# One plain group of heads instead of two, a second norm that ends later, and a rotation on folded rows, in a four-stage decoder step

## The chip, the core and the metric

The kernel runs on one core of a Trainium2 chip. The metric is device time of one execution, in microseconds: the median of repeated runs, with the lowest and highest. One further execution was taken with the hardware profiler, and all rows quoted come from it. PE is the matrix engine (TensorE), PEld its weight loads, DVE the vector engine, ACT the scalar engine, POOL GpSimd, SP the queue that issues most DMAs.

## The reference

One inference step of a two-layer decoder with a shared key/value projection between the layers: 1024 prompt positions and 8 single-position samples, model width 2048, all in float32.

```
# layer 0 (mixer A), for prompt and samples
z = x @ w_in_a;  u, gate = split(z)
d = multiscale_pool(u)                      # trailing means over 2, 4, 8, 16 positions, minus u
d = einsum('btgc,gce->btge', d, w_grp_a) * scale
h = layer_norm(ALPHA * x + (d * silu(gate)) @ w_out_a)
# shared keys and values, once
k, v = split(h @ w_kv);  k = rope_partial(k)        # first 16 of 64 dims of each head
# layer 1 (mixer B)
z = h @ w_in_b;  q = rope_partial(z[..., :2048]);  gate = z[..., 2048:]
s = q k^T / 8, masked to a sliding window of 128;  softmax with one learned sink per head
y = layer_norm(ALPHA * h + (softmax(s) v * silu(gate)) @ w_out_b)

rope_partial: out = [x1*cos - x2*sin, x2*cos + x1*sin, rest]      # x1, x2: 8 dims each
```

It returns y for prompt and samples, the pooling states, and the last 128 keys and values.

## The kernel before

**Layout.** Activations lie with channels on the 128 partitions and positions along the free axis. The positions are cut into two chunks: chunk 0 has 512, chunk 1 has 520 (512 and the 8 samples). Every stage is run for chunk 0 and then for chunk 1, in the order of the table `PHASES`: `ai` (projection, pooling, gate), `ao` (output projection and norm), `bi` (keys, values, queries, gates, attention), `bo` (output projection and norm).

**Products.** A float32 product is made of three reduced-precision ones: each weight block and each activation tile is split into a high half (a cast on ACT, L505 for weights) and a low half (a subtraction on DVE, L520), and PE adds high x high, high x low, low x high (L684, L685, L686). A stage multiplies in one of two ways. *Plain* (`unit`, L712 to L714): 48 matmuls of 512 columns for 128 output channels. *By seven* (`pair` and `seven`): two tiles of output channels at a time, by the Strassen-Winograd scheme, in seven products of 24 matmuls with half the columns (256 or 260). These seven need sums of weight blocks (a block of a pair of input tiles is 128 x 1024) and of activations. Weight sums are formed on DVE (L349) by `first_pair`, which in chunk 0 also stores them to DRAM (`swib`, by POOL, L351) for chunk 1, where `next_pair` loads them. The sums of activations are four DVE operations, `t_ops` (L895 to L898), stored by POOL (L899) as `th` for the norm's output and `to` for the attention's.

**The stage that changes.** `bi` for chunk 0, from 1077.1 to 1508.0 us. It first makes keys and values and the first two groups of heads plain (a group is two tiles of query channels and two of gate channels: four plain units or two pairs by seven), then six groups by seven. While it runs plain, the norm of `ao` for chunk 1 (`ln_gen`, c = 1) is done as side work: mean, then subtraction (L1031), squares (L1034) and their sums (L1037) for each of eight tiles of 2 x 520 columns, then a second pass that multiplies (L1071), applies gain and offset on ACT (L1060), stores `h`, and forms and stores the activations' sums `th`. The eight tiles stay in SBUF between the two passes. In chunk 1 the pairs in `FORM` (groups 0 and 1, whose sums chunk 0 never needed) form their sums themselves and do not store them.

**Rotation.** `w_kv` and `w_in_b` are permuted so that the two rotated halves of a head lie 32 partitions apart. `partner` copies a tile (or pair of tiles) into another with the 32-row blocks exchanged (four SP DMAs), and `rope` multiplies both by tables (L1740), and the sum is formed at L1848, all on the full 128 partitions and all columns.

**Attention** (`attend`) of one query tile is a chain of small steps hung on products that come later: scores (L1879), select (L1896), mask and maximum (L1900, L1904), exponentials (L1915), normalisation (L1928), transposes (L1932), copies (L1941, L1942), values (L1957), gate (L1966) and its store `o` (L1969), and for every second tile the `t_ops` and their store.

**What sets the order.** Every engine runs its instructions in the order in which the source records them (`in_order`). Time in the source is counted in products: `begin` opens one and `end` closes it, `self.at(n, go)` and `self.product(n, rank, go)` record `go` at the end of the n-th product from now, and one step of side work is taken there if enough memory is free (`every`, `room`). `begin` also keeps the weights ahead: it loads seven entries ahead, casts four and forms low halves for three, counted with the one that is opened, so that low halves lie two products ahead of PE:

```
a, b, d = self.ahead if self.strassen else (5, 4, 3)      # ahead = 7, 4, 3
self.load_to(self.e + a);  self.prep_to(self.e + d);  self.cast_to(self.e + b)
```

**Memory.** SBUF beyond the constants is one pool of 54 slots (`Mem`) of a block or a pair of tiles each. `full` and `half` take the whole slot that was released longest ago; a slot whose content was stored counts as ten releases younger. A writer of a slot waits until its last reader is done, a store by DMA too.

## Time and profile before

| | |
|---|---|
| median of 3 runs | 2302.97 us (2302.83 to 2305.52) |
| the profiled execution, its span | 2307.35 us, 2305.6 us |
| PE, DVE, ACT, POOL busy | 2281.9, 1942.7, 1388.5, 192.3 us |
| TensorE clock granted | 0.999 |
| `bi` chunk 0, plain part | 1077.1 to 1221.5 us: 144.4 us, PE 144.40, DVE 120.39 |
| `bi` chunk 0, by seven | 1221.5 to 1508.0 us: 286.5 us, PE 286.04, DVE 257.76 |
| `bi` chunk 1 begins | 1508.0 us |

A row of a group reads: line, engine, operation, output tile <- input tiles with their shapes, count, then busy us and mean ns of one, then the engine's idle time just before it and what ended it. A row of the waits reads: who waited, for whom, us in total, how many times, the longest. A tile named `m` is a slot of the pool, `pD`, `pS`, `pO` are PSUM banks.

### The profile page before, as it was taken

How to read it: one execution, taken by the hardware profiler on the slowest of the kernel's cores; microseconds unless marked ns; L12 is line 12 of the kernel's file. 1: busy time of each engine (PE TensorE's matmuls, PEld its weight loads, DVE VectorE, ACT ScalarE, POOL GpSimd, SP SyncE). 2: the span in 40 equal slices, each digit the busy share in tenths (PEclk: the TensorE clock that was granted, in tenths of full speed). 3: DMA queues.
4: the chain of work that ended last, by engine and by line, in shares of the span. 5: the costliest groups of instructions: out<-in, count | busy, mean ns of one | idle time of the engine just before them, and what ended most of it. 6: DMA issues, size and time to landing. Idle time of an engine off the chain costs nothing.

```text
span 2305.6 us, 50389 instructions
## 1 busy us (share of the span) xinstructions
PE 2281.9 (99%) x20353; PEld 2211.4 (96%) x20353; DVE 1942.7 (84%) x2415; ACT 1388.5 (60%) x2547; POOL 192.3 (8%) x359
## 2 busy tenths in 40 slices
PE   9999999999999999999999999999999999999998
PEld 8999999999999999999889999999999999999998
DVE  8888889877878878988878989899877777889997
ACT  5544446544546546555466776785766778656665
POOL 0111110011010000000001111100000000010001
PEclk9999999999999999999999999999999999999999
DMA  7779679988889989999667767787787778799894
GB/s 257 264 267 309 233 255 325 318 303 295 298 308 320 345 294 317 321 352 383 214 255 252 241 226 239 264 285 231 230 264 234 252 239 293 244 364 379 289 339 151
DMA packets 246394, 648.31 MB, mean 281 GB/s; under 512 B 25200, under 2 KB 106000, under 8 KB 246160
## 3 DMA queue, kind: packets, MB, share of 16 engines
q1 hardware_dynamic: 204288, 493.13, 64.1%
q0 software_dynamic: 41872, 151.96, 17.0%
q8 instruction: 159, 2.61, 0.5%
q14 instruction: 75, 0.61, 0.1%
HBM read 463.00 MB, written 172.47 MB: 276 GB/s over the span
## 4 chain that ended last, share of the span: by engine, by line
PE 54%; DVE 2%; DMA 2%; ACT 1%; issue 1%; SPq 0%; POOL 0%; DVEq 0%; POOLq 0%; ACTq 0%
PE pD L684 14%; PE pD L686 13%; PE pD L685 13%; PE pD L712 2%; PE pO L1957 2%; PE pD L714 2%; PE pD L713 2%; PE pS L1879 2%; PE pS L1932 1%; DMA m<-in_woa 1%; DVE m L520 1%; DMA h<-m 0%; DMA m<-swob 0%; PE pS L1957 0%; PE pO L684 0%
## 5 line engine op out<-in xcount | busy, mean ns | idle before, releaser
L684 PE MATMUL pD<-m,m 128*128 128x260 f32 (+1 forms) x5088 | 1440.6, 283 | 5.8 <-ACT pD L644 2.3
L686 PE MATMUL pD<-m,m 128*128 128x260 f32 (+1 forms) x5088 | 1433.4, 282 | 5.3 <-DVE m L520 5.2
L685 PE MATMUL pD<-m,m 128*128 128x260 f32 (+1 forms) x5088 | 1433.6, 282 | 0.0
L684 PEld LDWEIGHTS pD<-m,m 128*128 128x128 f32 x5088 | 958.3, 188 | 15.3 <-issue 6.2
L686 PEld LDWEIGHTS pD<-m,m 128*128 128x128 f32 x5088 | 958.8, 188 | 7.4 <-DVE m L520 7.4
L685 PEld LDWEIGHTS pD<-m,m 128*128 128x128 f32 x5088 | 958.0, 188 | 0.5
L520 DVE TENSOR_TENSOR m<-m,m 128x1024 fp32r<-128x1024 f32 x690 | 833.4, 1218 | 93.4 <-ACT m L505 37.9
L505 ACT CAST m<-m 128x1024 fp32r<-128x1024 f32 x690 | 720.8, 1049 | 264.2 <-DVE m L349 127.5
L349 DVE TENSOR_TENSOR m<-m,m 128x1024 f32<-128x1024 f32 x136 | 166.1, 1221 | 13.1 <-DMA m<-in_wia 10.7
L847 DVE TENSOR_TENSOR m<-m,m 128x1024 fp32r<-128x1024 f32 (+1 forms) x118 | 143.8, 1224 | 7.3 <-ACT m L838 5.7
L838 ACT CAST m<-m 128x1024 fp32r<-128x1024 f32 (+1 forms) x118 | 123.3, 1052 | 9.7 <-DVE m L520 3.9
L657 ACT COPY m<-pD 128x260 f32<-128x260 f32 (+1 forms) x88 | 32.9, 374 | 118.2 <-PE pD L686 117.9
L1915 ACT ACTIVATE m<-m,sm 128x128 f32<-128x128 f32 x256 | 99.3, 391 | 0.0
L645 DVE TENSOR_TENSOR m<-pD,m 128x260 f32<-128x260 f32 (+1 forms) x92 | 38.3, 416 | 69.9 <-ACT pD L644 63.8
L1181 PE MATMUL pD<-m,m 128*128 128x260 f32 (+1 forms) x528 | 91.5, 323 | 0.0
L623 ACT ACTIVATE pD<-pD 128x260 f32<-128x260 f32 (+1 forms) x90 | 33.3, 370 | 93.6 <-PE pD L686 93.3
L712 PE MATMUL pD<-m,m 128*128 128x512 f32 x224 | 89.1, 398 | 0.0
L714 PE MATMUL pD<-m,m 128*128 128x512 f32 x224 | 88.2, 394 | 0.0
L713 PE MATMUL pD<-m,m 128*128 128x512 f32 x224 | 88.1, 393 | 0.0
L1181 PEld LDWEIGHTS pD<-m,m 128*128 128x128 f32 x528 | 79.4, 188 | 8.2
L1928 ACT ACTIVATE m<-m,sm 128x128 f32<-128x128 f32 x256 | 81.9, 392 | 7.0 <-DVE sm L1923 6.3
L632 ACT COPY m<-pD 128x260 f32<-128x260 f32 (+1 forms) x92 | 34.3, 373 | 77.4 <-PE pD L686 77.2
(257 smaller groups left out, 2096.3 us busy)
## 6 DMA issues: line engine op xcount, KB each, us to landing
m<-in_wib SPq DMA_DIRECT2D x132, 512.0 KB
m<-in_wia SPq DMA_DIRECT2D x128, 512.0 KB
m<-swoa SPq DMA_DIRECT2D x64, 512.0 KB
swia<-m POOLq DMA_DIRECT2D x56, 512.0 KB, 4.7
m<-swia SPq DMA_DIRECT2D x56, 512.0 KB
m<-swob SPq DMA_DIRECT2D x56, 512.0 KB
m<-in_wob SPq DMA_DIRECT2D x52, 512.0 KB
m<-in_woa SPq DMA_DIRECT2D x48, 512.0 KB
```

The lines of the kernel that those rows point to most:

```text
L349: self.nc.vector.tensor_add(s[out].a[:, :1024], s[x].a[:, :1024], s[y].a[:, :1024])
L505: self.nc.scalar.copy(hi.r[:, :1024], self.stream[self.cast].src().a[:, :1024])
L520: self.nc.vector.tensor_sub(lo.r[:, :1024], s.src().a[:, :1024], hi.a[:, :1024])
L684: nc.tensor.matmul(ps[:, :TH], wh[:, s], h, start=new and k == 0, stop=False, skip_group_check=on)
L685: nc.tensor.matmul(ps[:, :TH], wh[:, s], l, start=False, stop=False, skip_group_check=on)
L686: nc.tensor.matmul(ps[:, :TH], wl[:, s], h, start=False, stop=k == 7, skip_group_check=on)
L712: nc.tensor.matmul(ps[:], wh[:, s], h, start=par == 0 and k == 0, stop=False)
L713: nc.tensor.matmul(ps[:], wh[:, s], l, start=False, stop=False)
L714: nc.tensor.matmul(ps[:], wl[:, s], h, start=False, stop=par == 1 and k == 7)
L838: self.nc.scalar.copy(h.r[:, :n], s.a[:, :n])
L847: self.nc.vector.tensor_sub(l.r[:, :n], s.a[:, :n], h.a[:, :n])
L1181: nc.tensor.matmul(ps[:, : cs.stop - cs.start], ws[:, s], d[:, cs], start=f0 and k == 0, stop=l0 and k == 3,)
```

## The change

It does the following.

- `PHASES`: plain in `bi` of chunk 0 are now only keys, values and group 0; seven groups go by seven. Group 1 there forms its weight sums and stores them, and in chunk 1 it loads them (`FORM` holds group 0 alone).
- `ln_gen` for chunk 1: after a tile has been centred and squared, it is stored (`p`) and its slot released; the second pass loads it again, and waits until the stage runs by seven. There it takes a step at every second product at most, if four slots are free.
- Rotation: the 16 rotated rows of each of the two heads in a tile are written to DRAM (SP), read back folded, so that eight pieces of the columns and eight rows lie on 64 partitions (SP), turned by three DVE operations on 128 x 256 elements, written back to DRAM (POOL), and read back into the tile (SP), at products 0, 1, 3 and 5 after the tile is done (0, 1, 2, 4 for the last). The permutation within a head is dropped, the tables are folded too. Keys are then copied by ACT.
- Scores, and all that hangs on them, come two products later; two decode steps three later, and decode scores lie elsewhere in the bank.
- `begin` keeps fewer entries ahead when fewer than three slots are free (in `bi`; fewer than five in `bo` of chunk 0).
- `acc` of `phase_out` is taken when it is first needed; the next stage's activations are begun in the last unit of values.

```diff
-    ("ai", 0, (0, 1)), ("ai", 0, (1, 8)), ("ai", 1, (0, 8)), ("ao", 0, None), ("ao", 1, None), ("bi", 0, (0, 2)),
-    ("bi", 0, (2, 8)), ("bi", 1, (0, 8)), ("bo", 0, None), ("bo", 1, None),
+    ("ai", 0, (0, 1)), ("ai", 0, (1, 8)), ("ai", 1, (0, 8)), ("ao", 0, None), ("ao", 1, None), ("bi", 0, (0, 1)),
+    ("bi", 0, (1, 8)), ("bi", 1, (0, 8)), ("bo", 0, None), ("bo", 1, None),
...
-FORM = (0, 1)
+FORM = (0,)
...
-DEC_AT = (0, 1, 6, 6, 7, 8, 9, 10, 13, 13), (11, 11, 12, 12, 13, 14, 15, 16, 17, 17)
+ROPE_AT = (0, 1, 3, 5), (0, 1, 2, 4)
+DEC_AT = (3, 4, 6, 6, 7, 8, 9, 10, 13, 13), (11, 11, 12, 12, 13, 14, 15, 16, 17, 17)
...
-        if getattr(self, "ph", "") == "bi1" and len(self.mem.whole()) < 3:
-            a, b, d = min(a, 6), min(b, 3), min(d, 2)
+        if getattr(self, "ph", "") in ("bi0", "bi1", "bo0") and len(self.mem.whole()) < (5 if self.ph == "bo0" else 3):
+            a, b, d = min(a, 5 if self.ph == "bo0" else 6), min(b, 3), min(d, 2)
...
                 if 1 <= p <= 8:
                     sqs[p - 1] = sq if p == 1 else self.mem.full(2 * T)
                     nc.scalar.activation(flat(sqs[p - 1]), flat(pre[p - 1]), AF.Square)
+                    nc.gpsimd.dma_start(away(p - 1), self.pair_view(pre[p - 1], T))
+                    pre.pop(p - 1).free(True)
...
+        while c == 1 and not self.strassen:
+            yield
...
+        if c == 1:
+            load(0)
+            yield
+            for p in range(8):
+                t = self.pair_view(pre[p], T)
+                nc.vector.tensor_mul(t, t, b2(rr))
+                affine(p)
+                load(p + 1)
+                yield
+                self.t_ops(t[:, 0], t[:, 1], td, p, T // 2)
+                pre[p].free(True)
+                yield
+            L.free()
+            return
...
+    def rope(self, s, n, T, last=False):
...
+        def out():
+            for j in range(2):
+                nc.sync.dma_start(rows[j], s.a[64 * j : 64 * j + 16, :N])
+
+        def take():
+            w = box["w"] = self.mem.half(4 * C)
+            for j in range(2):
+                nc.sync.dma_start(w.v(2, C)[64 * j : 64 * j + 64], packed[j])
+
+        def turn():
...
+            nc.vector.tensor_mul(y, x, tab[:, None, :C].to_broadcast([P, 2, C]))
+            nc.vector.tensor_mul(x, x, tab[:, C : 3 * C].rearrange("p (h c) -> p h c", h=2))
+            nc.vector.tensor_add(y, y, x[:, ::-1, :])
+            for j in range(2):
+                nc.gpsimd.dma_start(packed[j], y[64 * j : 64 * j + 64])
+
+        def back():
+            box.pop("w").free(True)
+            for j in range(2):
+                nc.sync.dma_start(s.a[64 * j : 64 * j + 16, :N], rows[j])
+
+        for k, go in zip(ROPE_AT[last], (out, take, turn, back)):
+            self.at(k, go)
...
-                at, s1, ticks = (12 + 7 * n, {12: 11, 13: 9}.get(t, 12), SPREAD) if t < 14 else (
-                    11 + 7 * n, {14: 10, 15: 8}[t], CLOSE
+                at, s1, ticks = (14 + 7 * n, {12: 11, 13: 9}.get(t, 12), SPREAD) if t < 14 else (
+                    13 + 7 * n, {14: 10, 15: 8}[t], CLOSE
...
+            elif (kind, c) == ("bi", 0):
+                self.every, self.room = 2, 4
```

In the rows that follow a slot of the pool is `m`, its number, then how many slots had been handed out and a running number: two names with the same first number are the same memory. First DVE in `bi` of chunk 0, by seven, where the attention's sums `to` of a pair of tiles (L895 to L898, now L898 to L901) are written into a slot that POOL then stores. Before, from the last of the four:

```order
L898 TENSOR_TENSOR m31_1870_16612<-m12_1845_16289,m31_1870_16612 128x256
L520 TENSOR_TENSOR m41_1873_16628<-m29_1851_16343,m17_1869_16584 128x1024
L1900 COPY_PREDICATED m47_1871_16622<-cst_76,pS_215_13088 128x1024
L1904 TENSOR_REDUCE sm_298_16658<-m47_1871_16622 128x8
L1907 SCALAR_TENSOR_TENSOR sm_299_16659<-sm_298_16658,prm_75 128x8
L1908 TENSOR_TENSOR sm_300_16660<-sm_299_16659,prm_75 128x8
L520 TENSOR_TENSOR m0_1877_16674<-m23_1861_16458,m19_1874_16630 128x1024
L349 TENSOR_TENSOR m23_1861_16458<-m23_1861_16458,m29_1851_16343 128x1024
L520 TENSOR_TENSOR m31_1882_16716<-m5_1854_16383,m43_1878_16676 128x1024
```

and now, from the norm's sums `th` (the last two of whose four operations are shown) to the rotation:

```order
L900 TENSOR_TENSOR m25_1834_16200<-m36_1750_15047,m25_1834_16200 128x260
L901 TENSOR_TENSOR m25_1834_16200<-m36_1750_15047,m25_1834_16200 128x260
L523 TENSOR_TENSOR m53_1838_16214<-m23_1811_15883,m19_1831_16089 128x1024
L523 TENSOR_TENSOR m21_1839_16216<-m28_1825_16034,m24_1837_16212 128x1024
L352 TENSOR_TENSOR m28_1825_16034<-m28_1825_16034,m23_1811_15883 128x1024
L2005 SCALAR_TENSOR_TENSOR m32_1816_15920<-pO_283_16147,m30_1746_15009 128x512
L898 TENSOR_TENSOR m0_1841_16249<-m32_1816_15920 128x256
L899 TENSOR_TENSOR m0_1841_16249<-m32_1816_15920 128x256
L900 TENSOR_TENSOR m0_1841_16249<-m32_1816_15920,m0_1841_16249 128x256
L901 TENSOR_TENSOR m0_1841_16249<-m32_1816_15920,m0_1841_16249 128x256
L523 TENSOR_TENSOR m0_1846_16270<-m11_1818_15965,m25_1840_16218 128x1024
L1939 COPY_PREDICATED m41_1842_16259<-cst_76,pS_215_13092 128x1024
```

Before, slot 31 is written again by the third low half after the sums; now slot 0 is written again by the first, and the norm's sums stand just ahead. The order has this first-after form three times, and the second-after form twice before it.

Second, POOL at the same place: before,

```order
L351 DMA swib12_137<-m5_1803_15730 128x1024
L351 DMA swib12_137<-m12_1800_15690 128x1024
L1969 DMA o0_88<-m17_1794_15636 128x512
L899 DMA to0_85<-m9_1819_15959 128x1024
L351 DMA swib12_137<-m34_1810_15805 128x1024
```

and now:

```order
L902 DMA th1_92<-m25_1834_16200 128x1040
L354 DMA swib12_141<-m28_1825_16034 128x1024
L2008 DMA o0_88<-m32_1816_15920 128x512
L902 DMA to0_85<-m0_1841_16249 128x1024
L1933 MEMSET m41_1842_16259 128x256
L1784 DMA rows3_102<-m30_1843_16262 64x2x128 x2
L354 DMA swib5_134<-m45_1845_16268 128x1024
```

The store of `th` and the rotation's rows have come into the queue around the gate's store `o` and the store of `to`.

Third, ACT at the same place, the casts (L508) of the weights:

```order
L626 ACTIVATE pD_284_16206<-pD_282_16122 128x256
L508 CAST m24_1837_16212<-m28_1825_16034 128x1024
L508 CAST m25_1840_16218<-m11_1818_15965 128x1024
L1967 ACTIVATE m37_1817_15927<-m37_1817_15927,sm_281_15960 128x128 x4
L1935 COPY m41_1842_16259<-pS_215_13092 128x768
L632 COPY m30_1843_16262<-pD_285_16222 128x256
L508 CAST m32_1847_16272<-m28_1825_16034 128x1024
```

The second cast now writes slot 25, from which `th` is being stored, and the third slot 32, from which `o` is; what it casts is the block whose low half DVE writes into slot 0 above.

124 lines of the change are left out of this document (60 added, 64 removed).

## The prediction

> **What bounds the kernel now.** I read the page's head first, then busy time by stage, then the waits of the stage that is changed.
>
> ```profile
> span 2305.6 us, 50389 instructions
> PE 2281.9 (99%) x20353; PEld 2211.4 (96%) x20353; DVE 1942.7 (84%) x2415; ACT 1388.5 (60%) x2547; POOL 192.3 (8%) x359
> ```
>
> TensorE is busy for 2281.9 of 2305.6 us, so only two things can move the time: fewer matmul columns, or PE made to wait. The table by stage shows the first stage's plain units alone, the first output projection (56 products by seven), and then the changed stage's plain part and part by seven, and the first 100 us of its second chunk.
>
> ```profile
> 30.10:52.30 22.20, 22.20 (x97) 1.00 0.50 169
> 750.70:909.90 159.20, 159.20 (x1352) 1.00 0.89 313
> ...
> 1077.10:1221.50 144.40, 144.40 (x834) 116.71 (x833) 120.39 (x152) 81.36 (x155) 12.90 (x25) 1.00 0.74 258
> 1221.50:1508.00 286.50, 286.04 (x3212) 278.68 (x3210) 257.76 (x301) 202.79 (x475) 37.65 (x75) 1.00 0.72 248
> 1508.00:1560.00 52.00, 52.00 (x522) 50.86 (x522) 48.78 (x58) 43.57 (x94) 2.67 (x5) 1.00 0.76 264
> 1560.00:1610.00 50.00, 49.77 (x475) 49.01 (x472) 47.89 (x61) 25.32 (x45) 3.26 (x5) 1.00 0.73 238
> ```
>
> (Columns of the four long rows: length, then busy us of PE, weight loads, DVE, ACT and POOL, the clock, the DMA share, GB/s.) The stage by seven holds six groups of heads in 286.5 us, 47.75 us a group; DVE works 257.76/6 = 42.96 of these and idles 4.8. PE waits 0.46 us in all of it. So PE sets the pace and DVE has a margin of a tenth. The last two rows show that DVE at 94 to 96% has cost PE 0.23 us in 102: a high DVE share alone is harmless. What DVE waits for is the next view, the waits in that stage, first of DVE, then of PE (there to the second chunk's end):
>
> ```profile
> DVE m L1942 <- ACT m L1941: 8.4, 5, 3.2
> DVE m L520 <- DMA to<-m: 5.8, 3, 2.3
> DVE m L520 <- ACT m L1915: 4.3, 3, 1.7
> ...
> PE pS L1879 <- DVE m L1848: 1.2, 1, 1.2
> ```
>
> The second row is the one that matters. L520 forms the low half of a weight block, the thing each product needs; three times it stood still until a store `to` had left the buffer that it wanted.
>
> **The matmuls.** Group 1 turns from 192 matmuls of 512 columns into 336 of 256. From the rows above a 512-column matmul issues every 22.20/96 = 0.231 us (a window counts one that reaches in) and a 256-column one every 159.20/1352 = 0.118 us. 192 x 0.231 = 44.4 against 336 x 0.118 = 39.6: **-4.8 us**, or -4.6 if only the 1344 matmuls of the products are counted in the second window. This is all that the change can win on PE, which has next to no waits to give back.
>
> **DVE's work in the stage by seven.** Rotation and norm change; their rows, first from the stage's groups, then from the whole program's by form:
>
> ```profile
> L1740 DVE TENSOR_TENSOR m<-m,m 128x1024 f32<-128x1024 f32 (+1 forms) x14 | 15.4, 1140 | 0.0
> L1848 DVE TENSOR_TENSOR m<-m,m 128x1024 f32<-128x1024 f32 (+1 forms) x7 | 8.0, 1149 | 0.2
> ...
> L1071 DVE TENSOR_TENSOR m<-m,m 128x1040 f32<-128x1040 f32 x8 | 9.8, 1235 | 0.0
> L895 DVE TENSOR_TENSOR m<-m 128x260 f32<-128x260 f32 x32 | 13.4, 420 | 2.0 <-PE pD L685 1.1 <-DMA m<-o 0.9
> L457 DVE TENSOR_TENSOR m<-m 128x256 f32<-128x256 f32 x56 | 23.4, 419 | 1.1
> ```
>
> Rotation of a pair was two multiplications and an addition, 3 x 1.15 = 3.4 us; on folded rows it is three operations of 256 columns, for which L457 is the nearest row: 3 x 0.42 = 1.3, so -2.1 a group. The norm's second pass moves in: per tile one multiplication (1.24) and the four operations of the transform (4 x 0.42), 2.9 us, eight tiles. In the new order they fall in the first five of the seven groups: 8 x 2.9/5 = +4.7 a group there. So DVE has 42.96 - 2.1 + 4.7 = 45.5 of 47.75, 2.2 us spare. By the rows of 1508 to 1610 that still costs nothing. ACT gets the affine and the copies of the keys; at 202.79 of 286.5 it has room. The stores and loads added (eight stores and eight loads of the centred tiles, eight stores of weight sums, in the second chunk six loads more) are some 12 MB beside 107 MB in these 431 us: the DMA share goes from 0.73 to about 0.81, and the output projection ran at 0.89 with PE never waiting. The eight sums that leave the second chunk (10 us of DVE) can return only the 0.23 us that PE waits there.
>
> **Where the change costs: buffers.** The norm's tiles, their transforms and the rows of the rotation now want slots of the same pool as the weights, and fewer are free. The order shows it: the transform `to` of a pair of heads was stored from a slot whose next writer was the third low half after it; now it is the very next one (three groups), before that the second (two groups). DVE executes in order, so it stands at that low half until the store has landed. How long that is, the trace of before shows: the store's landings in this stage, the norm's `th` (its own place, 970 to 1170 us), the weight sums', and DVE's timeline round one case.
>
> ```profile
> L899 POOL DMA_DIRECT2D to<-m x6: 533/533/542, 1229.9 to 1483.8; - x6
> ...
> DMA to landing us min/median/max: 5.4/7.7/9.6
> ...
> L899 POOL DMA_DIRECT2D th<-m x15: 533/533/547, 970.6 to 1169.8; - x15
> ...
> DMA to landing us min/median/max: 4.8/7.3/9.0
> ...
> L351 POOL DMA_DIRECT2D swib<-m x45: 531/533/547, 1227.8 to 1490.2; - x45
> ...
> DMA to landing us min/median/max: 2.9/4.5/8.2
> ```
>
> ```profile
> 1340.13 0.43 DVE L898 TENSOR_TENSOR m<-m,m 128x256 f32<-128x256 f32 x1
> 1340.47 1.22 DVE L520 TENSOR_TENSOR m<-m,m 128x1024 fp32r<-128x1024 f32 x1
> 1341.61 1.32 DVE L1900 COPY_PREDICATED m<-cst,pS 128x1024 f32<-128x1024 int32 x1
> ...
> 1344.50 1.22 DVE L520 TENSOR_TENSOR m<-m,m 128x1024 fp32r<-128x1024 f32 x1
> 1345.76 1.23 DVE L349 TENSOR_TENSOR m<-m,m 128x1024 f32<-128x1024 f32 x1
> 1348.81 2.36 DVE L520 TENSOR_TENSOR m<-m,m 128x1024 fp32r<-128x1024 f32 x2 [1.83 <-DMA to<-m]
> ```
>
> The transform ended at 1340.56 and the slot was free at 1348.81: 8.3 us, of which 6.4 were covered by two low halves, the mask, the maximum and a weight sum. In the new order nothing covers it: three stands of 8.3 us. Where one low half and one sum lie between (2.4 us) 5.9 remain, where a low half, a sum, the gate and the norm's multiplication lie between (4.8) 3.5. Together **34.3 us** in five groups. On ACT, in the same products, the cast of the same weight block waits for the slot of a `th` stored one step earlier; it ends about when DVE's stand does and I add nothing.
>
> Against it stand DVE's spare 5 x 2.2 = 11 us and its lead. The low half is formed two products ahead, at most 2 x 24 x 0.118 = 5.7 us, and this is used up once, since a DVE with 2.2 us spare a group hardly wins it back. 34.3 - 11 - 5.7 = **17.6 us** of waiting PE. Bounds: if the lead were whole again at each case, 3 x (8.3 - 5.7) + 0.2 = 8; if none of the spare time could be used, because it is itself waits such as those for ACT above, 34.3 - 5.7 = 29. I take 16.5, near the middle term, since PE's stops give DVE some lead back. The sum is -4.8 + 16.5 = **+11.7 us**. The profiled execution took 2307.35, its span 2305.6; the span would be 2317.3. The median of the runs shown is 2302.97, 4.4 under that execution, so I forecast 2314.7.
>
> The Trainium skill ("DMA: Bandwidth & Descriptors", section "Anatomy of one DMA — SWDGE (gpsimd) path") puts such a store at 2.0 us plus its bytes over 436 GB/s, an estimate of 3.2 us for 512 KB. By it the stands shrink to 3.6 us, which spare time and lead cover, and the sum is -4.8. The trace disagrees: the shortest of the six `to` took 5.4.
>
> **Rotation and score.** The rotation's path was one hop of SP copies, is now four (rows out, folded in, folded out by POOL, rows back), and SP waits in line at the second and fourth, with weight loads behind it. From rows out to the score lie seven products, 7 x 24 x 0.118 = 19.8 us; four hops at the landings shown (2.9 to 5 for small ones, 8 at most) are 12 to 20. So the score should find its rows, barely; missed by 1 us at each of 14 tiles it would cost 14. Before, PE waited there once for 1.2 us. I take 0, and leave the rest to the range.
>
> **Rivals.** (1) *The whole gain.* The stores land in about 3 us, or DVE runs further ahead than two products: -4.8, 2298.2. For it: weight sums landed in 2.9; PE has waited for almost nothing so far. Against: all six `to`, behind the gate's store and beside the loads, took 5.4 or more, and now a `th` goes just before. (2) *The stands eat the gain and no more.* Landings of 5.4 give stands of 5.8, 3.4 and 1.0: 21.8 us, less 11 and 5.7, is 5, and 5 - 4.8 is nothing: 2303. PE's stops would shorten the landings towards this. (3) *DVE and ACT stop in turn.* Casts late on ACT keep a bank's eviction, so that DVE's spare time is lost too, and SP's waits at the folded rows make loads late: 29 - 4.8 = +24, 2327. For it: nine casts of this stage take, in the new order, a slot whose store was issued in the same or the preceding product. Against: ACT is idle for 29% of the stage.
>
> **How the numbers follow.** Forecast 0.68, rival 1 0.12, rival 2 0.13, rival 3 0.07. The likeliest one's own range is 8 to 29 less 4.8: 2306 to 2327. The range that should hold 8 in 10 goes down to rival 1 and up past rival 3's figure: 2298 to 2328. A difference under 0.2% (4.6 us) can't be told from no change. Rival 1 lies at that bound and gives faster 0.11; same has the rest of it, rival 2, and the forecast's low end, 0.17; slower 0.72.
>
> **What would show it.** Right: in the stage by seven, DVE's low half (now L523) waits on DMA `to<-m` 3 times for some 8 us, DVE stays near 45 us a group, and PE waits for DVE's low half by 3 to 7 us in the third to fifth of the seven groups; groups six and seven take 47.7 us again; the matmuls of group 1 are 4.6 to 4.8 us shorter. By the Trainium skill ("Perfetto Trace Analysis", section "Optimization Strategy") a gap that repeats on the engine that should be full can mean too little memory for the next tile; here it would repeat once a group. Wrong: if these waits are there and PE stays at 47.7 a group, the lead was longer than two products; if they are under 4 us, the landing was; if PE waits at the scores for rows coming back, the rotation's path was too long, and the rest of my sum may still hold.

## The result: 3.3% slower

| | before | changed |
|---|---|---|
| median | 2303.76 us (2302.83 to 2305.52, 4 runs) | 2380.38 us (2378.25 to 2381.29, 4 runs) |
| ratio | | 1.033, 95% interval 1.0314 to 1.0345 |
| span of the profiled execution | 2305.6 us | 2379.2 us |
| TensorE clock granted, mean | 0.999 | 0.988 |

The forecast was +11.7 us, measured is +76.6. The direction was right, the size less than a sixth. The view by windows, cut at the stages of the changed kernel, shows where. Its columns are the stretch, its length, the busy time of PE, PEld, DVE, ACT and POOL, the granted TensorE clock, the DMA share and GB/s:

```profile
1073.00:1181.60 108.60, 96.35 (x470) 77.23 (x469) 75.88 (x85) 46.75 (x73) 15.63 (x28) 0.95 0.76 273
1181.60:1571.20 389.60, 351.88 (x3716) 338.68 (x3716) 300.63 (x379) 242.30 (x563) 56.04 (x107) 0.96 0.67 233
1571.20:2007.40 436.20, 435.11 (x4761) 425.19 (x4755) 324.39 (x449) 302.27 (x708) 38.32 (x60) 1.00 0.77 253
2007.40:2193.10 185.70, 177.21 (x1605) 174.50 (x1598) 156.31 (x191) 112.64 (x195) 13.97 (x26) 0.98 0.88 314
```

These are `bi` of the first chunk, plain and by seven, `bi` of the second chunk, and `bo` of the first. Length less PE's busy time is what PE waited: 12.3, 37.7, 1.1 and 8.5 us. The clock column gives the second loss. The records list 13 intervals at a clock of 0.5, 10.2, 34.1, 0 and 6.8 us in these four stretches. PE was busy for 5.0, 32.4, 0 and 6.7 us of them, and half of that is counted as lost; where PE waits, a low clock takes nothing more. What is left is PE's work at full clock. The same sum for both kernels, from first matmul to first matmul, in us:

| stage | before | changed | waits | lost to half clock | work |
|---|---|---|---|---|---|
| `ao`, chunk 1 | 167.6 | 163.6 | 4.2, now 0.4 | 0, 0 | 163.4, now 163.1 |
| `bi`, chunk 0 | 430.5 | 498.2 | 0.5, now 50.0 | 0, now 18.7 | 430.0, now 429.5 |
| `bi`, chunk 1 | 438.0 | 436.2 | 2.3, now 1.1 | 0, 0 | 435.7, now 435.1 |
| `bo`, chunk 0 | 174.0 | 185.7 | 0.6, now 8.5 | 0, now 3.4 | 173.3, now 173.8 |

So 57 us of new waits came in `bi` of chunk 0 and `bo`, and 22 us of half clock on top, while PE's own time in `bi` of chunk 0 shrank by 0.5 us and not by 4.8. From 1520 us on, when the norm is done, PE is busy for all of the stage's last 51.7 us. Who waited for whom in `bi` of chunk 0 (the view of waits: who, for whom, us in total, times, longest):

```profile
...
ACT m L508 <- DMA th<-m: 36.6, 6, 8.0
ACT m L508 <- DVE m L352: 27.6, 12, 6.8
DVE m L523 <- DMA to<-m: 20.1, 3, 6.9
DVE m L1780 <- DMA m<-rows: 18.3, 4, 14.5
ACT m L1067 <- DVE m L1075: 17.8, 8, 8.0
...
PE pD L687 <- ACT pD L647: 12.9, 6, 2.8
...
PE pD L687 <- ACT m L635: 11.0, 3, 4.0
...
PE pD L689 <- DVE m L523: 3.8, 5, 1.5
```

The third row is the forecast's: DVE's low half (L523) stands three times, 6.7 us each, for a store `to`. But PE hardly waits for the low half (last row). It waits for ACT to empty a PSUM bank (L647 copies it into another bank, L635 into a slot; both are called evictions below), and ACT stands longest in a cast (L508) whose slot holds a `th` on its way out. One such place, in the third group by seven, from the timelines of ACT, DVE and PE (start, duration, instruction, idle time before it and what ended it):

```profile
1331.54 1.05 ACT L508 CAST m<-m 128x1024 fp32r<-128x1024 f32 x1 [7.62 <-DMA th<-m]
...
1335.56 0.37 ACT L635 COPY m<-pD 128x256 f32<-128x256 f32 x1
```

```profile
1328.08 0.42 DVE L901 TENSOR_TENSOR m<-m,m 128x256 f32<-128x256 f32 x1
1335.01 1.23 DVE L523 TENSOR_TENSOR m<-m,m 128x1024 fp32r<-128x1024 f32 x1 [6.51 <-DMA to<-m]
```

```profile
1335.99 0.39 PE L687 MATMUL pD<-m,m 128*128 128x256 f32 x1 [3.58 <-ACT m L635]
```

DVE and ACT stand at once, for 3 us. The eviction L635 is queued on ACT behind the cast and the work that the cast held up, and PE waits for it. What the clock does just there (windows of PE alone: length, busy, clock, DMA):

```profile
1329.90:1333.30 3.40, 2.51 (x22) 1.00 1.03 405
1333.30:1336.70 3.40, 0.71 (x5) 1.00 0.54 164
1336.70:1340.10 3.40, 3.40 (x18) 0.50 0.00 0
1340.10:1343.50 3.40, 3.40 (x31) 1.00 0.50 152
```

After the wait PE is busy for the whole of the third window and does 18 matmuls where it does 31 in the fourth. In the kernel before, no such interval stands anywhere but in the last 7 us.

### The profile page after: what moved, and what is told of

The parts are those of the page before. It is cut to its first block, busy times and chain, and to the rows that moved or that the text cites. A ratio compares the mean times of both kernels' runs of the same rounds, so it can differ in the third digit from the quotient of the medians.

```text
span 2379.2 us, 50897 instructions
## 1 busy us (share of the span) xinstructions
PE 2303.1 (97%) x20497; PEld 2235.4 (94%) x20497; DVE 1913.8 (80%) x2419; ACT 1393.0 (59%) x2564; POOL 224.6 (9%) x413
## 5 line engine op out<-in xcount | busy, mean ns | idle before, releaser
L687 PE MATMUL pD<-m,m 128*128 128x260 f32 (+1 forms) x5200 | 1483.5, 285 | 41.2 <-ACT pD L647 12.9
L689 PE MATMUL pD<-m,m 128*128 128x260 f32 (+1 forms) x5200 | 1475.6, 284 | 11.4 <-DVE m L523 11.3
L688 PE MATMUL pD<-m,m 128*128 128x260 f32 (+1 forms) x5200 | 1474.0, 283 | 0.0
L687 PEld LDWEIGHTS pD<-m,m 128*128 128x128 f32 x5200 | 989.1, 190 | 54.1 <-ACT pD L647 14.3
L689 PEld LDWEIGHTS pD<-m,m 128*128 128x128 f32 x5200 | 989.2, 190 | 14.8 <-DVE m L523 14.5
L688 PEld LDWEIGHTS pD<-m,m 128*128 128x128 f32 x5200 | 989.1, 190 | 0.5
L523 DVE TENSOR_TENSOR m<-m,m 128x1024 fp32r<-128x1024 f32 x696 | 841.4, 1219 | 131.7 <-ACT m L508 49.9
L508 ACT CAST m<-m 128x1024 fp32r<-128x1024 f32 x696 | 725.8, 1048 | 263.7 <-DVE m L352 115.1
L660 ACT COPY m<-pD 128x260 f32<-128x260 f32 (+1 forms) x90 | 33.5, 372 | 126.2 <-PE pD L689 126.0
L1203 PE MATMUL pD<-m,m 128*128 128x260 f32 (+1 forms) x528 | 91.5, 323 | 0.0
L632 ACT COPY m<-pD 128x260 f32<-128x260 f32 (+1 forms) x92 | 34.3, 372 | 90.5 <-PE pD L689 83.0
L1203 PEld LDWEIGHTS pD<-m,m 128*128 128x128 f32 x528 | 79.4, 188 | 8.2
L635 ACT COPY m<-pD 128x260 f32<-128x260 f32 (+1 forms) x94 | 35.1, 374 | 84.9 <-PE pD L689 84.8
L647 ACT COPY pD<-pD 128x256 f32<-128x256 f32 (+1 forms) x80 | 28.8, 360 | 82.2 <-PE pD L689 82.0
L717 PE MATMUL pD<-m,m 128*128 128x512 f32 x160 | 63.9, 399 | 3.7 <-DVE m L523 3.7
```

What stands on the lines that cost most here:

```text
L508: self.nc.scalar.copy(hi.r[:, :1024], self.stream[self.cast].src().a[:, :1024])
L523: self.nc.vector.tensor_sub(lo.r[:, :1024], s.src().a[:, :1024], hi.a[:, :1024])
L687: nc.tensor.matmul(ps[:, :TH], wh[:, s], h, start=new and k == 0, stop=False, skip_group_check=on)
L688: nc.tensor.matmul(ps[:, :TH], wh[:, s], l, start=False, stop=False, skip_group_check=on)
L689: nc.tensor.matmul(ps[:, :TH], wl[:, s], h, start=False, stop=k == 7, skip_group_check=on)
L717: nc.tensor.matmul(ps[:], wl[:, s], h, start=False, stop=par == 1 and k == 7)
```

## The experiments

The theories as they stood. A: slots are written again behind their own store. B: the rotation's hops. C: the clock, each long wait costing more than its length. Later ones (Q, P, L, S, O, W and M) are stated in the expectations that test them. Every kernel is compared with runs of the kernel before on the same chip; its median there lay between 2303.7 and 2304.8.

### Which part of the change

**The rotation alone.** The rotation, its tables, the later scores and the later decode scores, with everything else in this stage as before:

```diff
-    ... ("bi", 0, (0, 1)), ("bi", 0, (1, 8)), ...        FORM = (0,)
+    ... ("bi", 0, (0, 2)), ("bi", 0, (2, 8)), ...        FORM = (0, 1)
...
-        while c == 1 and not self.strassen:
-            yield
```

> The kernel before with the new rotation alone: rows out to memory and folded back, scores two products later, the first chunk's decode scores three products later. Two plain groups, the norm's second pass inside them and the look-ahead rule stay as they were. Theory A (the time of the changed kernel goes into buffers that are written again behind their own store): in this kernel's order no buffer of the part by seven gets a new writer within two products of its store, against 15 in the changed kernel, so that part returns to about 47.7 us a group (the row before: 49.8, 45.2, 47.6, 47.6, 47.6, 48.7 for groups 2 to 7) and the whole to between 2303 and 2316, the upper end being the keys' 14.5-us stand of VectorE in the plain part if it stays with its 9.4 us of TensorE waits and 10 us at half clock. Theory B (the rotation's four hops and SyncE's waits for rows are the cause): the groups by seven stay at 53 to 58 us and the whole near 2370. The output projection of the first chunk (186.0 us in the changed kernel, 174.3 before) stays at 186 if the later decode scores are its cause, and returns to 174 if the look-ahead rule is.

2304.99 us, ratio 1.0004 (0.9994 to 1.0013): no difference. Its windows are the plain part, the part by seven (six groups) and `bo` of chunk 0:

```profile
1073.40:1216.80 143.40, 143.40 (x826) 115.83 (x825) 114.67 (x151) 78.80 (x142) 18.28 (x33) 1.00 0.76 258
1216.80:1503.50 286.70, 286.01 (x3218) 278.45 (x3216) 245.25 (x300) 203.81 (x482) 46.36 (x88) 1.00 0.72 246
1940.80:2119.90 179.10, 174.37 (x1596) 171.65 (x1597) 156.94 (x191) 114.75 (x196) 13.99 (x26) 1.00 0.91 326
```

PE never waits in the plain part and 0.7 us by seven, so theory B falls for the products by seven, and the keys' 14.5-us stand is not there either. Only `bo` has lost 5 us.

**The norm's second pass let go at once.** The same two lines `while ... yield` taken out of the changed kernel, nothing else:

> The changed kernel in all but one thing: the second pass of the second chunk's norm no longer waits for the products by seven, it runs as soon as the statistics are there, in the plain part and what follows. Rotation, one plain group and the look-ahead rule stay. Theory A: in the part by seven no buffer gets a new writer within two products of its store (15 such in the changed kernel), so its seven groups fall from 390 us to 334 to 340, and the whole from 2380 to some 2325 to 2335; the plain part keeps its 108 us or grows by a few, since 16 tiles' work of VectorE moves into it. Theory B (rotation): the seven groups stay near 390 and the whole near 2380. Theory C (half clock after each TensorE wait of 2.4 us or more) adds nothing of its own here, but wherever the waits go their windows of 3.41 us must go too: 41 us at half clock in the stage must fall to about 10.

2346.95 us, ratio 1.0186 (1.0171 to 1.0202). The part by seven takes 337.9 us with 2.8 us of waits, as A said: with the norm gone from it, seven groups wait for next to nothing. (The norm's stores and its work go together here; the runs below part them.) But the plain part grew to 127.7 us, where I had allowed a few. Its last wait:

```profile
1201.36 0.58 PE L687 MATMUL pD<-m,m 128*128 128x256 f32 x1 [18.89 <-ACT m L2181]
```

The eviction of the last gate stood on ACT behind casts and the norm's affine operations, which waited for DVE, which did three of the norm's transforms and two of its multiplications in those 18.9 us. The clock fell to half within the wait, for 20.5 us, of which PE stood 15.4. The cost moved with the norm.

### Slots behind their stores

**Giving slots back later.** In `t_ops`, and in the look-ahead rule so that the memory suffices:

```diff
-        s.free(True)
+        self.at(2, lambda: s.free(True))
...
-    ... len(self.mem.whole()) < (5 if self.ph == "bo0" else 3):
+    ... len(self.mem.whole()) < (5 if self.ph in ("bo0", "bi0") else 3):
```

> The changed kernel in all but this: in the part by seven a buffer that holds a transform on its way to memory is given back two products later than its store, and the look-ahead shrinks (6 loads, 3 casts, 2 low halves) when fewer than 5 instead of 3 buffers are free. The same instructions, the same norm by seven, the same rotation. Theory A: no writer stands behind a store any more (15 new writers within two products of a store become 1), so the waits of ScalarE's cast for `th` (36.6 us) and of VectorE's low half for `to` (20.1 us) go below 5 us each, the seven groups fall from 390 to between 334 and 350, the whole to between 2325 and 2345. Theory B: the seven groups stay near 390. If the shrunken look-ahead is itself a wait, they stay above 350 with TensorE waiting for low halves or casts whose buffers were long free.

2356.02 us, ratio 1.0224 (1.0209 to 1.0240), so -24.4 against the changed kernel. In its view of waits no row of ACT for `th` and none of DVE for `to` is left. The part by seven fell from 389.7 to 364.1 us: waits from 37.7 to 21.5, half clock from 34.1 to 13.7. A is shown as a cause, worth 16 us of waits and 10 us of clock; it is not the only one, since the whole stayed 11 us above the expected range. (The edit has two parts, which were not tried apart; the shorter look-ahead alone, in a kernel without the norm by seven, cost 2 us, as the run on the look-ahead shows.) What remained, I took apart in six runs. Part by seven of each, in us:

| kernel | whole | part by seven | PE's waits | at half clock |
|---|---|---|---|---|
| changed | 2380.4 | 389.7 | 37.7 | 34.1 |
| changed, norm's transforms left out | 2363.6 | 370.0 | 24.2 | 17.1 |
| slots held | 2356.0 | 364.1 | 21.5 | 13.7 |
| held, transforms left out | 2350.9 | 359.9 | 18.5 | 13.7 |
| held, affine left out | 2348.4 | 358.4 | 14.6 | 19.7 |
| held, all of the norm's work left out | 2344.3 | 354.0 | 12.6 | 17.1 |
| held, affine one step later | 2373.3 | 383.8 | 34.4 | 27.3 |

**The norm's transforms left out**, first with slots held, then with the slots of the changed kernel:

```diff
-        nc.vector.tensor_sub(t[:, 1, :], E[:, a], E[:, b])
-        ... (four operations)
+        if dst is self.Td.get(("h", 1)):
+            nc.gpsimd.memset(s.a[:, : 4 * TH], 0.0)
+        else:
+            ... (four operations)
```

> The kernel with buffers given back two products after their store (2356.0, part by seven 364.1 us with 21.5 us of TensorE waits and 13.7 us at half clock), and one thing left out: VectorE does not form the transforms of the norm's eight tiles (4 operations of 0.42 us each), GpSimd fills them with zeros instead, so the second chunk's projection is computed from zeros and the outputs of that chunk aren't the reference's. Loads, stores, buffers and ScalarE's work stay. Theory L (after the store waits have gone, VectorE's and ScalarE's added work in the part by seven is what TensorE still waits for): 1.7 us less of VectorE per tile, waits below 10 us and half clock below 4 us, the part by seven 345 to 350 and the whole near 2340. Theory S (the shorter look-ahead of that kernel is what it waits for): the part by seven stays at 360 to 366 and the whole at 2354 to 2358.

> The changed kernel with the same work left out (the norm's transforms are filled with zeros by GpSimd, so the outputs of the second chunk aren't the reference's), and its buffers as they are. If buffers behind their stores were the whole cause in the part by seven, 389.7 us stay within some 5 us and the whole at 2375 to 2380, with ScalarE's cast still waiting about 36 us for `th` and VectorE's low half 20 us for `to`. If VectorE's load shares the blame, as theory L has it, the part by seven falls to 370 to 380 and the whole to 2360 to 2370.

Held: 2350.87, waits 18.5. That is between the two expectations, nearer S: five microseconds for eight transforms. With the slots of the changed kernel: 2363.63, and the view of waits there has

```profile
ACT m L508 <- DMA th<-m: 14.0, 4, 4.0
DVE m L523 <- DMA to<-m: 6.8, 2, 4.7
```

The stores are the same, but 1.7 us less of DVE per tile took more than half of the waits behind them. So work and store waits are not two separate sums. My reading, which no run shows by itself, is that a DVE that is less behind puts its stores out earlier, so that the next writer comes later after them.

**The look-ahead.** The shorter one forced on the kernel of the rotation alone:

```diff
+        if self.ph == "bi0" and self.strassen:
+            a, b, d = 6, 3, 2
         self.load_to(self.e + a)
```

> The kernel of the rotation alone (2305.0, part by seven 286.6 us with 0.7 us of TensorE waits), with the shorter look-ahead (6 loads, 3 casts, 2 low halves) forced on every product of the part by seven, and no norm in it. Theory S: TensorE waits for low halves and casts, some 15 us or more in six groups, part by seven 300 or more, the whole 2318 or more. Theory O: a look-ahead of two products is enough where no one is held up, waits stay below 4 us and the whole at 2304 to 2310.

2307.10, ratio 1.0016 (1.0006 to 1.0025), part by seven 289.7 with 2.7 us of waits. S falls for a part by seven without the norm; with it, the shorter look-ahead was not tried alone.

**The affine one step later**, in the kernel with slots held:

```diff
                 nc.vector.tensor_mul(t, t, b2(rr))
-                affine(p)
                 load(p + 1)
                 yield
+                affine(p)
+                yield
                 self.t_ops(t[:, 0], t[:, 1], td, p, T // 2)
```

> The kernel with buffers given back two products after their store (2356.0), and one order changed: the norm's affine operations on ScalarE are issued one step (two products) after VectorE's multiplication that they read, not right behind it. There ScalarE stood 19.5 us in six waits at the affine for a multiplication that was still queued on VectorE, and the evictions behind it kept TensorE. Theory O (two engines that each run in order wait for one another): the affine's waits fall below 5 us, TensorE's waits in the part by seven from 21.5 to 8 to 13 us, the half clock from 13.7 to below 7, the whole to 2338 to 2345. Theory S (the short look-ahead): nothing of it, 2353 to 2359.

2373.27, ratio 1.0305: slower by 17 us where I expected faster by 11 to 18. The wait that I aimed at is gone, and another has grown. First the kernel with slots held, then this one, same view and window:

```profile
ACT m L509 <- DVE m L353: 39.9, 15, 6.8
ACT m L1074 <- DVE m L1082: 19.5, 6, 8.0
```

```profile
ACT m L509 <- DVE m L353: 47.3, 14, 6.8
```

A cast that needs a weight sum now waits longer for DVE. PE's own waits grew behind ACT's copies ahead of the attention's values (from 4.7 to 14.0 us) and behind low halves (from 5.3 to 11.5). With three steps per tile the norm also lasts longer: its last multiplication came at 1340 us there, at 1451 here, so more groups have it in them. Whether that is why the time rose was not tried apart, so this run does not settle theory O: its gain did not come, but the affine's place and the norm's length changed together.

**All of the norm's work, then only its affine, left out** (the eight `tensor_mul`, the sixteen affine operations, the transforms; loads and stores kept):

> The kernel with buffers given back two products after their store (2356.0, part by seven 364.1 us, TensorE waits 21.5, half clock 13.7), with all of the norm's second pass on the engines left out: no multiplication on VectorE, no affine on ScalarE, no transform (GpSimd fills it with zeros). The loads, the stores, the buffers and their times of release stay, and so does the look-ahead. The second chunk's projection is computed from zeros. Theory W (the norm's work on two engines that run in order is what TensorE still waits for): waits below 6 us, half clock below 4, the part by seven 338 to 345, the whole 2330 to 2337. Theory M (its buffers and its transfers, through the look-ahead that shrinks when fewer than 5 are free): waits stay above 14 us, the part by seven above 355, the whole above 2346.

> The same kernel (2356.0) with the affine of the norm alone left out (16 operations of ScalarE; the second chunk's projection is computed from tiles without scale and offset), the multiplication and the transform on VectorE kept. The run without the transforms took 2350.9. If ScalarE is the engine that holds up the rest: waits in the part by seven fall from 21.5 to 12 or less and the whole to 2340 to 2346. If it takes both engines' work, or neither matters: 2350 to 2358.

2344.25 (ratio 1.0169) and 2348.42 (1.0190). Without any of the norm's work 12.6 us of waits stay, between W and M: 9 of the 21.5 us go with the work, 12.6 with something else. Leaving out the affine alone takes 6.9 us of waits, between the two cases of its expectation, so ACT's share of the norm's work does reach PE. Of the 12.6 us one wait of 4.8 us has DVE at the rotation's rows (5.84 us, behind two weight loads in SP's queue). The first product by seven waits another 3.3 us behind the last gate's eviction, just ahead of the part by seven and so counted in the plain part. That wait stands in every kernel of this study with one plain group. For the rest no single cause was found, and it stays open.

### The keys' rows

The keys' rotation in the changed kernel, from the timeline of SP's queue, and for comparison that of the rotation alone:

```profile
1091.07 0.32 SPq L997 DMA_DIRECT2D m<-p  x1
1092.98 0.33 SPq L288 DMA_DIRECT2D m<-in_wib  x1
1093.42 0.62 SPq L997 DMA_DIRECT2D m<-p  x1
1094.64 0.37 SPq L831 DMA_DIRECT2D m<-h  x1
1098.54 0.37 SPq L831 DMA_DIRECT2D m<-th  x1
1099.00 0.62 SPq L288 DMA_DIRECT2D m<-in_wib  x1
1099.71 2.41 SPq L1769 DMA_DIRECT2D rows<-m  x2
1114.84 0.64 SPq L1774 DMA_DIRECT2D m<-rows  x1
```

```profile
1092.01 2.91 SPq L997 DMA_DIRECT2D m<-p  x2
1097.60 0.33 SPq L288 DMA_DIRECT2D m<-in_wib  x1
1098.21 1.22 SPq L1750 DMA_DIRECT2D rows<-m  x2
1103.05 0.64 SPq L1755 DMA_DIRECT2D m<-rows  x1
```

The read back (L1774) waits for the write (L1769) to land: 12.7 us from the end of its issue, against 3.6. Ahead of the write stand six loads of 512 and 520 KB within 9 us, against three in the kernel of the rotation. Two of the six (L831) are for the products by seven, which the change begins in the last unit of values. The edit begins them with the first query tile:

```diff
-                    if len(ps) == 1 and j == 1 and done == self.v_done:
-                        self.x_begin(nxt)
...
-                if t == 2 * ps[-1] - 1:
+                if t == max(2 * ps[-1] - 1, 0):
                     self.x_begin(nxt)
```

> The changed kernel, but the loads of the first activation tiles for the products by seven begin with the first query tile and not with the values' tile, about 24 us later. Theory Q (the keys' rows stand behind these loads in SyncE's queue: five loads of 512 KB within 9 us ahead of them): the rows land in some 5 us and not 12.6 (4.8 in the kernel of the rotation alone), VectorE's 14.5-us stand at the turned keys falls below 6, the plain part loses most of its 12.3 us of TensorE waits and its 10.2 us at half clock, and the whole goes to 2364 to 2370. Theory P (the eight stores of centred tiles that the change adds there fill the transfer engines, 397 GB/s between 1085 and 1095 us): rows and stand as they are, 2380.

2368.33 us, ratio 1.0281 (1.0267 to 1.0295): -12.0, as expected of Q. The plain part went from 108.6 to 99.5 us, with no half clock in it:

```profile
1072.70:1172.20 99.50, 93.88 (x471) 75.56 (x469) 75.74 (x85) 46.66 (x73) 15.62 (x28) 1.00 0.85 306
```

The rows now landed 7.1 us after the end of their issue, and DVE's longest stand at the keys' rows fell from 14.5 to 8.7 us, not below 6 as expected. That the two loads are a cause, worth the 12 us, is shown; the rest of the stand is not explained by them. How much the eight stores of centred tiles add (transfers ran at 397 GB/s there, 326 in the kernel of the rotation) was not tried apart.

### The output projection

Two edits touch it, the decode scores' place and the look-ahead rule. The first was undone in the kernel of the rotation alone, both in the changed kernel. With the scores at their old place they read the decode queries before the last pair is turned, so these two kernels' outputs for the samples aren't the reference's; the instructions are the same.

```diff
-DEC_AT = (3, 4, 6, 6, 7, 8, 9, 10, 13, 13), ...
+DEC_AT = (0, 1, 6, 6, 7, 8, 9, 10, 13, 13), ...
```

> The kernel of the rotation alone (new rotation, else the kernel before), with the first chunk-end's decode scores back at their old places (0 and 1 products after their base, not 3 and 4). If the later decode scores cost what that kernel lost in the output projection of the first chunk (179.1 us against 174.0, with 4.7 us of TensorE waits against 0.6), that stage returns to 174 and the whole is 2305.0 - 4 to 5 = 2300 to 2301, which would be under the kernel before (2304.2), since the waits of 2.3 and 1.4 us that the kernel before has in the output projection ahead of this stage are gone here. If the rotation's rows cost it, the stage stays at 179 and the whole at 2305.

```diff
-        if getattr(self, "ph", "") in ("bi0", "bi1", "bo0") and ...
+        if getattr(self, "ph", "") in ("bi0", "bi1") and ...
```

> The changed kernel with two things undone: the first decode scores at their old places, and the look-ahead rule without its case for the first chunk's output projection (fewer than 5 free buffers). If these two cost that stage its 11.7 us (185.7 against 174.0: 8.5 us of TensorE waits and 6.8 us at half clock against 0.6 and 0), it returns to 174 to 176 and the whole goes from 2380 to 2369, the stage by seven staying at 390. By the kernel of the rotation alone, the later scores would be 5 of it and the rule 7. If neither is the cause: 2380.

The first: 2306.89, ratio 1.0016 (1.0007 to 1.0026), `bo` 178.4 us. The decode scores are not the cause. The second: 2375.02, ratio 1.0311, `bo` from 185.7 to 177.4 us, waits 3.5 and no half clock. By the two, the rule costs some 8 us of the 11.7, though the whole fell by only 5.4. All kernels with the later scores have a row that the kernel before has not, DVE waiting for the stored attention output of the last heads; the changed kernel and that of the rotation alone:

```profile
DVE m L929 <- DMA o<-m: 3.9, 1, 3.9
```

```profile
DVE m L929 <- DMA o<-m: 2.9, 1, 2.9
```

The last gate comes two products later, and the next stage reads it at the old time. This would be the other 3 to 5 us; it was not tried.

### Together, and the running sum's buffer

Slots held, loads later, and the rule without `bo`:

> The changed kernel with three things mended at once: buffers given back two products after their store (alone 2356.0, so -24.4), the activation loads of the part by seven begun a query tile later (alone 2368.3, -12.0), and the look-ahead rule without its case for the first chunk's output projection (with the decode scores moved too: 2375.0, -5.4). If they are separate causes they add: 2380.4 - 24.4 - 12.0 - 5.4 = 2338.6, with a tolerance of 4. If the later loads only move the wait from the keys to the first product by seven (4.8 us there in the run alone), it is nearer 2345.

2343.65, ratio 1.0176 (1.0162 to 1.0191): -36.7 of the 41.8 that the single runs add up to. They are separate causes but for 5 us, of which 4 are clock: the part by seven ran 21.7 us at half clock here, 13.7 with slots held alone, its first product waiting 5.1 us and not 3.3. Then with the affine later and the norm on every third product (`self.every, self.room = 3, 4`):

> The kernel with the three things mended (2343.7), the affine one step later as above, and the norm's steps on every third product and not every second, so that its eight tiles spread over five groups by seven. If theory O holds, the two take most of the 20.4 us of waits and 21.7 us at half clock in the part by seven: 2343.7 - 12 to 22 = 2322 to 2332. If neither matters: 2340 to 2346. In no case does it come under the kernel before (2304): the 174 us of the output projection and the 95 of the plain part are not reached.

2360.04, ratio 1.0244: 16 us slower, about what the affine's own run had. Spreading the norm over more groups was no help.

The kernel before with one edit, `acc` taken when first needed:

> The kernel before with one line of thought of the change alone: the running sum of the output projections takes its buffer when the first two tiles are added, not at the stage's start. All kernels that have it ran the second chunk's output projection ahead of this stage in 163.6 us, the kernel before in 167.6, with two TensorE waits of 2.3 and 1.4 us that the others don't show. If this edit is why, and nothing else changes: 2303.7 - 4 = 2299.7, 0.17% under the kernel before. If those waits came from elsewhere (or are only one execution's): 2303.7, no difference.

2305.03, ratio 1.0004 (0.9995 to 1.0013): no difference, though its profile too has 163.6 us in `ao` of chunk 1 and not 167.6. The 4 us were those of the one profiled execution of the kernel before (2307.35 against a median of 2304), or come back elsewhere. No version that beats both kernels was found; the rotation alone equals the kernel before.

### The clock

The kernel before with 20 made waits in `ai` of chunk 1:

```diff
+        touch = lambda: nc.tensor.matmul(ps[:, :64], z.r[:, :P], z.r[:, P : P + 64], start=True, stop=True)
+        touch()
+        for cols in GAPS[n - 1]:
+            nc.gpsimd.memset(z.a[:, :cols], 0.0)
+        touch()
```

with `GAPS = [(1024,) * 3] * 20`, then `[(1024,)] * 20`.

> The kernel before with 20 made waits of TensorE in the input projection of the second chunk (every sixth product): a small matmul reads a tile of zeros, GpSimd writes it three times (128x1024, 0.95 us each in the profile before), a small matmul reads it again. Nothing else waits for this. Each wait should be about 3.05 us. If a wait costs its own length and no more: 20 x 3.05 = 61, so 2303 + 61 = 2364. Theory C (a wait of 2.4 us or more is followed by 3.41 us at half clock, as in the changed kernel's rows): 20 x (3.05 + 1.7) = 95, so 2398, with some 68 us at granted clock 0.5 in that stage, where the kernel before has none.

> The kernel before with the same 20 made waits as in the experiment on the clock, but GpSimd writes the tile once and not three times, so each wait is about 1.25 us (3.15 less two writes of 0.95) and some 0.9 us beside four of them. Theory C, sharpened by that run (there the clock fell only after a stretch of 3.41 us on a fixed grid in which TensorE had idled for more than about 1.8 us, and stayed low for one or two such stretches): no stretch holds 1.8 us of idle time, the clock stays at 1.0, and the time is 2304.2 + 20 x 1.25 + 3.5 = 2333. If instead every wait costs a fixed 2.7 us beside its length, as that run would also allow (125.5 us for 20 waits of 3.6): 2304 + 20 x 3.95 + 3.5 = 2387.

Three writes: 2429.74 us, +125.5, ratio 1.0548 (1.0532 to 1.0564). Waits and clock round one of them:

```profile
PE pO L576 <- POOL m L579: 72.0, 20, 5.9
```

```profile
438.20:441.60 3.40, 3.40 (x30) 1.00 0.61 155
441.60:445.00 3.40, 0.69 (x7) 1.00 0.78 304
445.00:448.40 3.40, 2.96 (x13) 0.50 0.43 113
448.40:451.80 3.40, 3.40 (x18) 0.50 0.96 320
451.80:455.20 3.40, 3.40 (x30) 1.00 0.48 140
```

All 20 waits were followed by half clock, 9 by one stretch of 3.41 us and 11 by two: 105.8 us, in 87.9 of which PE was busy, so 44 us lost beside 72.0 + 3.4 us of waits. That is 119 of the 125.5. With a wait that costs its length alone, it would have been +75.

One write: 2350.94 us, +47.2, ratio 1.0206 (1.0192 to 1.0220), where I had +29. The waits were 25.2 us as made. But the clock fell four times in that stage:

```profile
577.00:581.00 4.00, 4.00 (x36) 1.00 0.59 145
...
583.60:587.00 3.40, 1.91 (x14) 1.00 1.00 404
587.00:590.40 3.40, 3.40 (x18) 0.50 0.98 397
```

At three places a made wait of 1.49 us closely followed one of 0.86 us. The grid cut these pairs differently: the stretches of 3.41 us ahead of the half clock hold 1.50, 1.80 and 2.05 us of idle time (the row from 583.60 is the first of them, with the made wait alone in it). With one after a wait of 1.9 us and one more in a later stage, 17.1 us ran at half clock, 8.5 lost. Some 8 us more are PE's own time in that stage (40 small matmuls, and, as I take it, the restart after each wait), and 3.3 are waits in a later stage. So the expectation failed twice: I had looked at the waits one by one, and its limit of 1.8 us of idle time did not hold.

## Why the prediction was wrong

**The matmuls, -4.8: right for the matmuls, but not in the changed kernel's time.** With the norm let go at once, where the part by seven waits only 2.8 us, PE's work at full clock in the stage is 425.0 us, 5.0 less than before. In the changed kernel it is 429.5, only 0.5 less. The plain part's work is nearly the same in both (93.8 and 94.2 us), so the difference lies in the part by seven (335.8 against 330.8), which has the many waits; what PE's longer time beside them consists of was not taken apart.

**DVE's work, "costs nothing": wrong.** The load was sized well (42.9 us of DVE per group by the second window row, against 45.5 in five groups and 40.9 in two, 44.2 in the mean). But leaving out the transforms alone gave back 17 us, and with slots held the norm's work still makes 9 of 21.5 us of waits. A mean of 45 in 47.75 says nothing of the products in which it falls: of the norm's eight multiplications four came within the first 84 of 390 us, between 1208 and 1265, the last at 1460.

**Buffers, +16.5: the size met by chance, the path wrong.** Three stands of DVE came, 6.7 us each where I had 8.3. With such waits taken away PE's waits fell by 16.2 us. But they reached PE through ACT. The failing step is the one on ACT's cast, "it ends about when DVE's stand does and I add nothing": ACT stood 36.6 us at these casts, with the evictions behind it, and PE waited 11.0 and 12.9 us for evictions, 3.8 for low halves. I costed the stand and not the queue behind it.

**Rotation and score, 0: right by seven, wrong for the keys.** The rotation alone costs nothing that can be measured. The four hops were priced by landings of 512-KB stores (2.9 to 5 us). In the plain part its rows went out behind loads that the change had moved ahead of them; I had looked at the hops and not at what stands before them in SP's queue. That was 12 us.

**`bo` and the look-ahead rule, not in the sum:** 11.7 us, of which the rule some 8.

**The clock, not in the sum:** 22 us, over a quarter of the loss. Every wait was priced at its own length. The Trainium skill ("TensorE: Matmul & The Clock Gate", section "Part 1: The HAM clock gate") has a free-running window of about 3.4 us and half clock after an idle one; the trace agrees on the 3.41 us and on the half (a granted clock of 0.5), though here a stretch with 1.9 us of idle time was always enough. The Trainium skill's rule of thumb on the same page, no idle gaps over some 3.4 us ("HAM oscillation — how this bites in real kernels"), would have let pass the waits ahead of 7 of the 13 intervals, 2.25 to 3.28 us long; the measurement decides, and once 1.50 us of idle time in a stretch was enough.

By terms: -0.5 work, +49.5 waits in `bi` of chunk 0 (16 behind stores, 9 at the keys, the rest the norm's work and what is open), +18.7 clock there, +11.7 in `bo`, -1.8 in `bi` of chunk 1, -4.0 in `ao`: 73.6, as the spans differ. Rival 3, "DVE and ACT stop in turn", had the mechanism and was given 0.07 and a third of its price. Its objection, ACT idle for 29% of the stage, was the mistake of the forecast in small: an engine that runs in order can be idle and late at once.

The best mended version is still 39 us over the kernel before, since the part by seven keeps 20.4 us of waits and 10.5 us of clock, plain and `bo` some 11 of waits.

## What to carry to other kernels

When an instruction will stand, list what is queued behind it on the same engine and who waits for that; here the evictions behind a standing cast cost more than the cast. Work that is hidden by its mean load should be placed by product, not by group, and when a load is moved earlier, ask which small transfer now goes out behind it. Price a TensorE wait by the clock as well: in the changed kernel each microsecond of new waiting cost another 0.4 (22 us beside 57).

## What the hardware showed that was not expected

The granted clock is decided on a fixed grid of 3.41 us. Over the 19 traces (both kernels and 17 experiments), idle time of PE was added up in each stretch of that grid that ran at full clock: of more than 12,000 stretches with less than 1.5 us idle none was followed by half clock, of 102 with more than 1.9 us all were, and of 45 in between 14. Matmul ends are modelled, so the border is no sharper than that. It is the sum in a stretch that counts, not one wait, and a wait of 1.9 to 3.4 us costs more or nothing more by where it falls on the grid. At half clock a matmul of 256 columns takes 0.217 us on average from start to start where it takes 0.119 at full clock.

A write of 64 KB landed 12.7 us after its issue when six loads of half a megabyte had gone out on the same queue in the 9 us before, 7.1 us after it with four, and 3.6 us after it with three. In the kernel with three the transfers were also fewer (326 GB/s between 1085 and 1095 us, against 397 in the changed kernel), so how much the queue alone does is not shown.
